# A hybrid attention trunk in fp32 on one core: block products chained in PSUM in the channel mixers, modulation sums in rows of 512 and moved to the first mixer

## The chip, the core and the metric

One core of a Trainium2 chip runs the whole kernel. The metric is device time in microseconds (us), the median of several executions; smaller is better. The engines are called here as in the profile: PE (TensorE, matrix products), DVE (VectorE), ACT (ScalarE), POOL (GpSimd) and SP (SyncE, which in this kernel issues all transfers).

## The reference, cut to what matters

The input x is 1 x 1024 x 1024 in float32. Two layers each run a token mixer (layer 0: softmax attention with forgetting; layer 1: gated linear attention) and a channel mixer. A conditioning vector c modulates every sub-layer with six vectors of 1024 per layer: shift, scale and gate of the token mixer (j = 0, 1, 2) and of the channel mixer (j = 3, 4, 5).

```python
c_act = jax.nn.silu(c)
for i in range(2):
    mod = c_act @ ada_w[i] + ada_b[i]              # 1024 -> 6 * 1024
    sh1, sc1, g1, sh2, sc2, g2 = jnp.split(mod, 6, axis=-1)
    h = modulate(rms_norm(x, norm1_g[i]), sh1, sc1)
    y = forgetting_attention(h, ...) if i == 0 else gated_linear_attention(h, ...)
    x = x + g1[:, None, :] * y
    h = modulate(rms_norm(x, norm2_g[i]), sh2, sc2)
    gate, up = jnp.split(h @ ffn_w_in[i], 2, axis=-1)
    x = x + g2[:, None, :] * ((jax.nn.silu(gate) * up) @ ffn_w_out[i])
return rms_norm(x, final_g)
```

The hidden width of the channel mixer is 2816.

## The kernel before, in words

**Products.** Everything is float32. An operand is split into a high part (a copy rounded to PE's fp32r format, made by ACT, line 174) and a low part (the difference, made by DVE, line 175); a product is three matmuls, high by high, high by low and low by high, added in one PSUM bank (`mm3`, lines 285 to 288).

**Order.** The program is written in one order, and a scheduler with a model of time then places each engine's instructions; each engine runs its own in the order so found. Some edges are fixed by hand with `issue_after`.

**Channel mixer.** `ffn` (from line 1380) works in blocks of 2 x 2: the activations are cut into B11, B12, B21, B22 (4 x 128 rows by 512 tokens), the weights likewise, and seven block products replace eight, with sums of blocks as operands: T1 to T4 on the side of the activations, made once, and sums of weight blocks, made by POOL for each group (lines 876, 877, 878, 888, 894). A *group* is one pair of 128-column weight strips: kind 0 for the gate, kind 1 for up; eleven of each, alternating. The first group of each kind is computed plainly (`plain_tile`), the other twenty with seven products (the loop from line 1678). A product (`prod`, line 1548) is 12 matmuls of 128 x 512 into a bank taken from a ring of five. Before the change each product leaves its bank at once: ACT copies the first to C11 (line 1684), DVE adds each of the others to one or two of the four results C11, C12, C21, C22 in SBUF (`add`, line 1557, L1559). Seven adds and one copy make a group. `fin` (line 1540) then applies silu on ACT (kind 0, L1543) or multiplies gate by up on POOL (kind 1, L1545), and `hid_done` sends the hidden block to memory some products later (split again at L1419 and L1420). The weight operands (`feed`) sit in a ring of six tiles and are loaded and split up to five ahead.

**Modulation.** The sum c_act @ ada_w is not done on PE, but on DVE: rows of ada_w are loaded to partitions, and each instruction multiplies a tile by a column of c_act (one value per partition) and adds it to an accumulator (`ada_steps`, lines 447 to 481; L475 the first, L477 the rest). Before the change a tile holds 32 rows of ada_w, each cut in four strips of 256 columns that lie on four groups of 32 partitions, so 32 instructions of 256 columns make one (layer, j), with four transfers per step (`ada_load`, L414). `ada_end` (L420) then sums over the partitions with two small matmuls against a constant of four columns, and DVE adds ada_b (L423).

When each (layer, j) is computed: (0, 0) and (0, 1) at the start by code that does not change; (0, 2), (0, 3), (0, 4) on DVE during attention, in steps of four rows per partition, paced by `ada0(2.4)` in `qk_proj`; (0, 5) on POOL during attention (`ada_pool`, L438 and L440), paced by `ada0p`; (1, 0) and (1, 1) in the first channel mixer, where each product gives a share of time to `ada1`; (1, 2), (1, 3), (1, 4) in the gated linear attention by `ada1(5.1)` after each projection; (1, 5) in the second channel mixer. `Pace` (line 483) counts the time given and lets the generators run as far as it reaches; `ADA_A` and `ADA_B` are the costs charged for one step.

**Attention** (L1165 to L1226): scores on PE, minimum and sum on DVE (L1171), exponential on ACT (L1175), reciprocal on DVE (L1176), scaling on POOL (L1177), transposes on PE (L1197), products with v (L1209, L1211). The projections of the next pair of heads are woven in between. **Gated linear attention**: per head, gates on ACT and DVE (L1891 to L1914), projections of k, q, v and r, and a chain of chunk states (from line 1948).

Of the kernel before, what the change touches and what calls it, by code (L numbers as in the profile page):

```python
# [53 lines left out]
def trunk(ctx, tc, x, c, ada_w, ada_b, norm1_g, norm2_g, ffn_w_in, ffn_w_out,  # L54
# [111 lines left out]
    four = cst.tile([P, 4], F32, name="four")  # L166
    nc.vector.memset(four, 0.0)
    for q in range(4):
        nc.vector.memset(four[32 * q:32 * q + 32, q:q + 1], 1.0)
# [115 lines left out]
    def mm3(ps, ah, al, bh, bl, start, stop):  # L285
        nc.tensor.matmul(ps, ah, bh, start=start, stop=False)  # L286
        nc.tensor.matmul(ps, ah, bl, start=False, stop=False)  # L287
        nc.tensor.matmul(ps, al, bh, start=False, stop=stop)  # L288
# [84 lines left out]
    crep = [crt[0:8, psl(t)] for t in range(4)] + [mrows[4][0:16, :], mrows[5][0:16, :]]  # L373
    for t in range(6):
        nt, src = (4, rows2[0:8, :]) if t < 4 else (2, crow)
        nc.vector.tensor_copy(crep[t].rearrange("n (q r) -> n q r", q=4),
                              src.rearrange("n (r t) -> n t r", t=nt)[:, t % 4].unsqueeze(1)
                              .to_broadcast([src.shape[0], 4, 32]))
    vps = mp0([P, 224], F32, "vps")
    vec = cst.tile([P, 160], F32, name="vec")  # L380
    cact = cst.tile([P, 8], F32, name="cact")
    c42 = cst.tile([P, 64], F32, name="c42")

    def vec_rows():
        nc.tensor.transpose(vps[:, 0:P], rows, ident)
        for t in range(6):
            n, o = (8, 160 + 8 * t) if t < 4 else (16, 128 + 16 * t)
            nc.tensor.transpose(vps[:, o:o + n], crep[t], ident[0:n, 0:n])
# [22 lines left out]
    def ada_load(raw, l, j, n, nt):  # L411
        src = ada_w[l, 32 * nt * n:32 * nt * (n + 1), j * D:(j + 1) * D]
        for q in range(4):
            nc.sync.dma_start(raw[32 * q:32 * q + 32],  # L414
                              src[:, 256 * q:256 * q + 256].rearrange("(r t) c -> r t c", t=nt))

    def ada_end(l, j, acc):
        mp = pj([P, 2, 4], F32, f"mp{l}{j}")
        for b in range(2):
            nc.tensor.matmul(mp[:, b], acc[:, psl(b)], four, start=True, stop=True)  # L420
        o = l * 48 + j * 8
        qb = lambda t: t.rearrange("p (q b) -> p b q", b=2)
# [5 lines left out]
    def ada_pool(l, j, acc, raw):  # L428

        raw = raw.rearrange("p (t c) -> p t c", t=2)  # L430
        ada_load(raw, l, j, 0, 2)
        yield 1.0
        for n in range(16):
            for t in range(2):
                o = 32 + t * 16 + n
                y = raw[:, t] if n or t else acc
                with tc.issue_after(last_of("G")):
                    nc.gpsimd.tensor_scalar(y, raw[:, t], c42[:, o:o + 1], 1.0, op0=ALU.mult, op1=ALU.mult)  # L438
                    if n or t:
                        nc.gpsimd.tensor_add(acc, acc, y)  # L440
                if t and n < 15:
                    ada_load(raw, l, j, n + 1, 2)
                yield 1.0
        ada_end(l, j, acc)
        yield 1.0

    def ada_steps(l, j, acc, raw_of, nt, ahead):


        steps, got = deque(range(32 // nt)), deque()  # L450

        def load():
            if not steps:
                return
            n = steps.popleft()
            raw = raw_of([P, nt * 256], F32, f"ada{l}{j}{n}").rearrange("p (t c) -> p t c", t=nt)
# [5 lines left out]
        for n in range(32 // nt):  # L462
            load()
            if ahead:
                yield ADA_A
            raw = got.popleft()
            with ExitStack() as es:
                if ahead:
                    es.enter_context(tc.issue_after(last_of("D")))
                elif n == 0:  # L470
                    es.enter_context(tc.issue_after(split_after["D"]))
                for t in range(nt):
                    o = (0 if nt == 4 else 32) + t * (32 // nt) + n
                    if n == t == 0:
                        nc.vector.tensor_scalar(acc, raw[:, t], c42[:, o:o + 1], None, op0=ALU.mult)  # L475
                    else:
                        nc.vector.scalar_tensor_tensor(acc, raw[:, t], c42[:, o:o + 1], acc,  # L477
                                                       op0=ALU.mult, op1=ALU.add)
            yield ADA_B if ahead else 1.0
        ada_end(l, j, acc)  # L480
        yield 1.0

# [22 lines left out]
    ada0, ada0p, ada1 = Pace(), Pace(), Pace()  # L505

    def ada1_queue(js, acc, raws_):
        r = Cycle(raws_)
        for j in js:
            ada1.q.append(ada_steps(1, j, acc, r, 2, len(raws_) - 1))  # L510
# [497 lines left out]
    nc.scalar.activation(c42, vps[:, 160:224], AF.Silu)  # L1008
# [121 lines left out]
    def qk_proj(p, i):  # L1130
# [9 lines left out]
        if p > 1:  # L1140
            ada0(2.4)
# [98 lines left out]
    def attention(p):  # L1240
        for a in range(2):
            for g in ORDER:
                u = (p, a, g)
                lps = yield from scores(u)
                if p:
                    ada0p(0.8)
# [29 lines left out]
    ada0p.flush()  # L1276
# [103 lines left out]
    def ffn(l, oh, xs, slots, nm, mid, norm_end, each=None):  # L1380
# [153 lines left out]
        TMP = {(0, 0): 0, (0, 1): 1, (1, 1): 2, (1, 0): 0}  # L1534
# [5 lines left out]
        def fin(G, key):  # L1540
            d = gate_view(G.i, key)
            if G.kind == 0:
                nc.scalar.activation(d, d, AF.Silu)  # L1543
                return
            nc.gpsimd.tensor_mul(d, d, dest(G, key))  # L1545
            hid_done(G.i, key)

        def prod(w, t):
            ps = pin([P, HALF], F32, f"p{l}")
            n = len(t)  # L1550
            for k in range(n):
                mm3(ps, w.hi[:, k, :], w.lo[:, k, :], hi(t[k]), lo(t[k]), k == 0, k == n - 1)
# [4 lines left out]
        def add(G, key, ps, src=None):  # L1557
            d = dest(G, key)
            nc.vector.tensor_add(d, d if src is None else dest(G, src), ps)  # L1559
# [118 lines left out]
        for X in gs[2:]:  # L1678
# [5 lines left out]
            nc.scalar.copy(dest(X, C11), prod(feed.next(), B11))  # L1684
            p5 = prod(feed.next(), T1)
            up(8)
            add(X, C12, prod(feed.next(), T2), C11)
# [114 lines left out]
    def mid(*js):  # L1802
        v = Views(slots["hid"], 2, [HALF], f"ad{js[0]}").v
        ada1_queue(js, v[0][:, 0:256], v[1:4])

    ADA_A, ADA_B = 6.0, 3.0
    ffn(0, oh, xs, slots, "fo", lambda: mid(0, 1), norm_mixer)
# [11 lines left out]
    vr = Ring(big, take(5))  # L1819
# [10 lines left out]
    ada_v = Views(take(2), 2, [HALF], "ad").v  # L1830
    ada1_queue((2, 3, 4), ada_v[0][:, 0:256], ada_v[1:3])
    ADA_A, ADA_B = 2.6, 1.0
    rm = ada_v[3]
# [33 lines left out]
    def gv_body(h, wv, tp, behind=None):  # L1867
# [5 lines left out]
        if h:  # L1873
            ada1(5.1)
# [43 lines left out]
    def head_front(h, b16, t2, ei, nmid):  # L1918
# [4 lines left out]
        for hf in range(2):  # L1923
# [3 lines left out]
            ada1(5.1)  # L1927
# [9 lines left out]
        for hf in range(2):  # L1937
# [3 lines left out]
            ada1(5.1)  # L1941
# [92 lines left out]
    def r_proj(h, gs, done):  # L2034
        wr_ = [None, None]
        for hf, dv in ((0, 0), (0, 1), (1, 0), (1, 1)) if h else ((0, 0), (1, 0), (0, 1), (1, 1)):
# [4 lines left out]
            ada1(5.1)  # L2041
# [58 lines left out]
    ada1.flush()  # L2100
# [50 lines left out]
    ffn(1, oh, xs, slots, "go", lambda: mid(5), final_norm, final_scale)  # L2151
# [30 lines left out]
```

## Time and profile before

| | us |
|---|---|
| median of 3 runs | 2394.64 |
| lowest and highest | 2393.22, 2395.78 |
| span of the profiled execution, first to last instruction | 2392.7 |

Only the span of the profiled execution is given, not its device time; the median of the runs is 1.9 us above it.

The stages by the profile's clock: loads, norm and first projections 0 to 95; attention 95 to 610; its output and the norm 610 to 686; first channel mixer, the seven-product groups with modulation 686 to 1040, the rest to 1310; gated linear attention 1310 to 1712; output and norm to 1768; second channel mixer 1768 to 2345; last norm and stores to 2393. A view by stages gives, for each stretch, its length, the busy time of each engine with its number of instructions, the granted TensorE clock (1.00 is full speed), the busy share of the DMA engines and the rate. A group's row has line, engine, operation, the tiles (out<-in), the shape, the count, then busy us and mean ns of one, then idle time before them and what ended it. In a chain or a timeline a row has start, length, and what ran.

### The profile page before, as it was taken

What the parts mean: (1) busy time and instruction counts of PE and PEld (TensorE: products, weight loads), DVE (VectorE), ACT (ScalarE), POOL (GpSimd) and SP (SyncE); (2) the same over time, 40 slices, a digit from 0 to 9 for tenths busy, and PEclk for the clock granted to TensorE, in tenths of its full rate; (3) what the DMA queues carried; (4) which work ended last, traced back from release to release, by engine and by line L of the source; (5) the groups of instructions that cost most, each with busy time, mean ns of one, the idle gap of its engine ahead of it and who ended that gap; (6) DMA issues with size and microseconds to landing.
All of it is one profiled execution on the core that took longest, in us unless ns stands there. A gap on an engine that the chain in (4) does not pass through costs nothing.

```text
span 2392.7 us, 35859 instructions
## 1 busy us (share of the span) xinstructions
PE 2367.3 (99%) x12344; PEld 2017.8 (84%) x12344; DVE 1770.0 (74%) x2984; ACT 1127.9 (47%) x2164; POOL 1046.2 (44%) x974
## 2 busy tenths in 40 slices
PE   8999999999999999999999999999999999999998
PEld 7888888888888888888888888898888888888888
DVE  6577787876698788876798565655687878775787
ACT  6656565664443333345325545453343334345326
POOL 1334444533446666643264221222345666643262
PEclk9999999999999999999999999999999999999999
DMA  7423333342435545457655242334424544457664
GB/s 254 151 79 112 102 119 93 121 142 78 150 113 178 176 162 168 168 203 266 223 183 161 68 119 87 100 113 132 143 99 154 183 150 154 154 186 258 227 199 147
DMA packets 336286, 363.43 MB, mean 152 GB/s; under 512 B 24860, under 2 KB 277944, under 8 KB 336104
## 3 DMA queue, kind: packets, MB, share of 16 engines
q1 hardware_dynamic: 336104, 361.15, 46.2%
q8 instruction: 97, 1.59, 0.3%
q14 instruction: 85, 0.70, 0.1%
HBM read 268.19 MB, written 92.86 MB: 151 GB/s over the span
## 4 chain that ended last, share of the span: by engine, by line
PE 89%; DVE 3%; DMA 3%; ACT 2%; issue 1%; SPq 1%; POOL 0%; DVEq 0%; POOLq 0%; ACTq 0%
PE p_b L288 16%; PE p_b L286 16%; PE p_b L287 16%; PE o_b L1211 2%; PE t_b L1197 2%; PE qk_b L286 2%; PE qk_b L287 2%; PE qk_b L288 2%; PE vps_b L288 1%; PE vps_b L286 1%; PE vps_b L287 1%; PE gr_b L286 1%; PE gr_b L287 1%; PE gr_b L288 1%; PE s_b L1165 1%; PE s_b L1166 1%
## 5 line engine op out<-in xcount | busy, mean ns | idle before, releaser
L175 DVE TENSOR_TENSOR o_s<-xv_s,o_s 128x512 fp32r<-128x512 f32 (+1 forms) x376 | 324.4, 868 | 62.8 <-ACT o_s L174 62.4
L174 ACT CAST o_s<-xv_s 128x512 fp32r<-128x512 f32 (+1 forms) x376 | 216.1, 587 | 293.9 <-PE p_b L288 242.3
L287 PE MATMUL p_b<-B,o_s 128*128 128x512 f32 x608 | 237.5, 391 | 0.0
L288 PE MATMUL p_b<-B,o_s 128*128 128x512 f32 x608 | 236.9, 390 | 0.0
L286 PE MATMUL p_b<-B,o_s 128*128 128x512 f32 x608 | 235.6, 391 | 0.0
L876 POOL TENSOR_TENSOR ex_s<-xv_s,xv_s 128x512 f32<-128x512 f32 (+1 forms) x64 | 86.8, 1357 | 288.0 <-DMA xv_s<-in_ffn_w_in_dram 118.2
L1177 POOL TENSOR_SCALAR lp_s<-lp_s,st 128x128 f32<-128x128 f32 (+7 forms) x128 | 97.5, 765 | 248.9 <-DVE st L1176 227.2
L286 PE MATMUL p_b<-T,o_s 128*128 128x512 f32 x480 | 186.7, 389 | 0.0
L287 PE MATMUL p_b<-T,o_s 128*128 128x512 f32 x480 | 186.7, 389 | 0.0
L288 PE MATMUL p_b<-T,o_s 128*128 128x512 f32 x480 | 181.2, 389 | 0.0
L288 PEld LDWEIGHTS p_b<-B,o_s 128*128 128x128 f32 x608 | 114.5, 188 | 23.8
L286 PEld LDWEIGHTS p_b<-B,o_s 128*128 128x128 f32 x608 | 114.6, 188 | 23.8
L287 PEld LDWEIGHTS p_b<-B,o_s 128*128 128x128 f32 x608 | 114.5, 188 | 23.8
L1175 ACT ACTIVATE lp_s<-lp_s,st 128x128 f32<-128x128 f32 (+7 forms) x128 | 99.3, 777 | 61.9 <-DVE st L1171 60.0
L878 POOL TENSOR_TENSOR xv_s<-ex_s,xv_s 128x512 f32<-128x512 f32 (+1 forms) x64 | 87.6, 1368 | 60.8 <-DVE o_s L175 58.2
L174 ACT CAST pt_s<-t_b 128x512 fp32r<-128x512 f32 (+1 forms) x160 | 79.8, 547 | 72.0 <-PE t_b L1197 71.4
L1559 DVE TENSOR_TENSOR ex_s<-ex_s,p_b 128x512 f32<-128x512 f32 x140 | 93.6, 680 | 25.1 <-PE p_b L288 24.9
L227 POOL TENSOR_TENSOR w_l_s<-w__s,w_h_s 128x256 fp32r<-128x256 f32 x90 | 69.3, 798 | 91.1 <-ACT w_h_s L223 51.9
L175 DVE TENSOR_TENSOR pt_s<-t_b,pt_s 128x512 fp32r<-128x512 f32 (+1 forms) x160 | 96.3, 630 | 15.7 <-ACT pt_s L174 15.2
L287 PEld LDWEIGHTS p_b<-T,o_s 128*128 128x128 f32 x480 | 90.1, 188 | 18.7
L286 PEld LDWEIGHTS p_b<-T,o_s 128*128 128x128 f32 x480 | 90.1, 188 | 18.7
L288 PEld LDWEIGHTS p_b<-T,o_s 128*128 128x128 f32 x480 | 90.1, 188 | 18.6
(1956 smaller groups left out, 7427.6 us busy)
## 6 DMA issues: line engine op xcount, KB each, us to landing
xv_s<-in_ffn_w_in_dram SPq DMA_DIRECT2D x176, 256.0 KB, 3.4
hid_B<-x SPq DMA_DIRECT2D x70, 512.0 KB, 2.9
ad_s<-in_ada_w_dram SPq DMA_DIRECT2D x384, 64.0 KB, 2.4
hid_T<-x SPq DMA_DIRECT2D x36, 512.0 KB, 2.9
xv_s<-in_ffn_w_out_dram SPq DMA_DIRECT2D x96, 192.0 KB, 5.0
ada_s<-in_ada_w_dram SPq DMA_DIRECT2D x96, 128.0 KB, 2.9
xv_s<-in_ffn_w_out_dram SPq DMA_DIRECT2D x40, 256.0 KB, 2.9
T2o<-hid_T SPq DMA_DIRECT2D x18, 512.0 KB, 8.8
```

What stands on the lines that cost most here:

```text
L174: nc.scalar.copy(hi, src)
L175: nc.vector.tensor_sub(lo, src, hi.bitcast(F32))
L227: (nc.gpsimd if i < 3 else nc.vector).tensor_sub(lo[:, cs], rw[:, cs], hi[:, cs].bitcast(F32))
L286: nc.tensor.matmul(ps, ah, bh, start=start, stop=False)
L287: nc.tensor.matmul(ps, ah, bl, start=False, stop=False)
L288: nc.tensor.matmul(ps, al, bh, start=False, stop=stop)
L876: nc.gpsimd.tensor_add(s1, a21, a22)
L878: nc.gpsimd.tensor_sub(a11, s1, a11)
L1175: nc.scalar.activation(lp, lp, AF.Exp, bias=mcur, scale=-1.0, accum_out=st[:, qi, 2:3])
L1177: nc.gpsimd.tensor_scalar(lp, lp, st[:, qi, 3:4], 1.0, op0=ALU.mult, op1=ALU.mult)
L1197: nc.tensor.transpose(tp[:, i, :], lps[qi][:, psl(2 * b + jj)], ident)
L1559: nc.vector.tensor_add(d, d if src is None else dest(G, src), ps)
```

## The change

In the channel mixers a product may go on in the bank of an earlier one. The bank `a` takes B11, T2, T3 and T4 in turn and is read after each; the bank `d` takes T1 and then B22. C11, C22 and C12 are first filled by ACT copies (three per group), three adds on DVE are left (C11, C22, C12), and C21 never lies in SBUF as a partial sum: kind 0 applies silu straight from the bank, kind 1 multiplies from the bank on DVE. A group takes three banks of the ring, not seven. The product with B22 is written ahead of that with T4, and two weight blocks change places in the order of loading.

Modulation tiles hold 64 rows by 512 columns on two groups of 64 partitions, so 16 instructions of 512 columns make one (layer, j), with two transfers per step; the constant has two columns, and the end takes four matmuls. POOL's sum is gone. (0, 5) and (1, 0) to (1, 4) are computed in the first channel mixer, with four buffers for raw rows in place of three; (0, 2) to (0, 4) stay in attention, in steps of two rows per partition; (1, 5) stays in the second channel mixer. In the gated linear attention the two slots that fall free give one more buffer for v.

```diff
     def ada_load(raw, l, j, n, nt):
-        src = ada_w[l, 32 * nt * n:32 * nt * (n + 1), j * D:(j + 1) * D]
-        for q in range(4):
-            nc.sync.dma_start(raw[32 * q:32 * q + 32],
-                              src[:, 256 * q:256 * q + 256].rearrange("(r t) c -> r t c", t=nt))
+        src = ada_w[l, 64 * nt * n:64 * nt * (n + 1), j * D:(j + 1) * D]
+        for q in range(2):
+            nc.sync.dma_start(raw[64 * q:64 * q + 64], src[:, hsl(q)].rearrange("(t r) c -> r t c", r=64))
 
     def ada_end(l, j, acc):
-        mp = pj([P, 2, 4], F32, f"mp{l}{j}")
-        for b in range(2):
-            nc.tensor.matmul(mp[:, b], acc[:, psl(b)], four, start=True, stop=True)
+        mp = pj([P, 4, 2], F32, f"mp{l}{j}")
+        for b in range(4):
+            nc.tensor.matmul(mp[:, b], acc[:, psl(b)], two, start=True, stop=True)
...
             yield ADA_B if ahead else 1.0
+        yield 5.0 if ahead else 1.0
         ada_end(l, j, acc)
...
-                r += [blk(a, A11), (op_a12, l, a), blk(a, A21, *then), blk(a, A22), blk(a, A12)]
+                r += [blk(a, A11), (op_a12, l, a), blk(a, A21, *then), blk(a, A12), blk(a, A22)]
...
-            ada0(2.4)
+            ada0(2.6)
...
-    acc0 = acc_r([P, 2, HALF], F32, "acc0")
-    ada0p.q.append(ada_pool(0, 5, acc0[:, 0, 256:512], acc0[:, 1]))
-    acc0 = acc0[:, 0, 0:256]
+    acc0 = acc_r([P, HALF], F32, "acc0")
     for j in (2, 3, 4):
-        ada0.q.append(ada_steps(0, j, acc0, wr, 4, 0))
+        ada0.q.append(ada_steps(0, j, acc0, wr, 2, 0))
...
-        def fin(G, key):
+        def fin(G, key, ps=None):
             d = gate_view(G.i, key)
             if G.kind == 0:
-                nc.scalar.activation(d, d, AF.Silu)
+                nc.scalar.activation(d, d if ps is None else ps, AF.Silu)
                 return
-            nc.gpsimd.tensor_mul(d, d, dest(G, key))
+            if ps is None:
+                nc.gpsimd.tensor_mul(d, d, dest(G, key))
+            else:
+                nc.vector.tensor_mul(d, d, ps)
             hid_done(G.i, key)
...
-            nc.scalar.copy(dest(X, C11), prod(feed.next(), B11))
-            p5 = prod(feed.next(), T1)
+            a = prod(feed.next(), B11)
+            nc.scalar.copy(dest(X, C11), a)
+            d = prod(feed.next(), T1)
+            nc.scalar.copy(dest(X, C22), d)
             up(8)
-            add(X, C12, prod(feed.next(), T2), C11)
+            prod(feed.next(), T2, a)
+            nc.scalar.copy(dest(X, C12), a)
             up(11)
             add(X, C11, prod(feed.next(), B21))
             fin(X, C11)
-            add(X, C22, prod(feed.next(), T3), C12)
-            add(X, C12, p5)
+            prod(feed.next(), T3, a)
+            add(X, C22, a)
+            fin(X, C22)
             up(15)
-            add(X, C21, prod(feed.next(), T4), C22)
-            fin(X, C21)
-            add(X, C22, p5)
-            fin(X, C22)
+            prod(feed.next(), B22, d)
+            add(X, C12, d)
+            fin(X, C12)
+            prod(feed.next(), T4, a)
+            fin(X, C21, a)
             up(20)
-            add(X, C12, prod(feed.next(), B22))
-            fin(X, C12)
             up(21)
...
-    ADA_A, ADA_B = 6.0, 3.0
-    ffn(0, oh, xs, slots, "fo", lambda: mid(0, 1), norm_mixer)
+    ADA_A, ADA_B = 2.0, 1.0
+    ffn(0, oh, xs, slots, "fo", lambda: mid(0, (0, 5), *((1, j) for j in range(5))), norm_mixer)
...
-    vr = Ring(big, take(5))
+    vr = Ring(big, take(6))
```

The calls `ada1(5.1)` after the projections of the gated linear attention are taken out, `ada_pool` and `ada0p` with them. `prod` takes an optional bank and then starts no new sum in it. At the start, one transposed block with c on 16 rows replaces six.

More of the change, by code (lines that the diff above doesn't have):

```diff
@@ L165, in trunk @@
     nc.vector.memset(mhalf, -0.5)
-    four = cst.tile([P, 4], F32, name="four")
-    nc.vector.memset(four, 0.0)
-    for q in range(4):
-        nc.vector.memset(four[32 * q:32 * q + 32, q:q + 1], 1.0)
+    two = cst.tile([P, 2], F32, name="two")
+    nc.vector.memset(two, 0.0)
+    for q in range(2):
+        nc.vector.memset(two[64 * q:64 * q + 64, q:q + 1], 1.0)
     maskb = cst.tile([P, P], BF16, name="maskb")
@@ L283, in next, with mm3 @@
             return self.got.popleft()
[L285 to L288, printed above, removed]
+    def mm3(ps, ah, al, bh, bl, start, stop, more=False):
+        nc.tensor.matmul(ps, ah, bh, start=start, stop=False, skip_group_check=more)
+        nc.tensor.matmul(ps, ah, bl, start=False, stop=False, skip_group_check=more)
+        nc.tensor.matmul(ps, al, bh, start=False, stop=stop, skip_group_check=more)
     def proj(ps, w, hs, hf):
@@ L426, in ada_end @@
                 make_a(l, i)
[L428 to L445, printed above, removed]
     def ada_steps(l, j, acc, raw_of, nt, ahead):
-        steps, got = deque(range(32 // nt)), deque()
+        steps, got = deque(range(16 // nt)), deque()
         def load():
@@ L461, in ada_steps @@
             load()
-        for n in range(32 // nt):
+        for n in range(16 // nt):
             load()
@@ L1555, in prod, with add @@
             return ps
-        def add(G, key, ps, src=None):
+        def add(G, key, ps):
             d = dest(G, key)
-            nc.vector.tensor_add(d, d if src is None else dest(G, src), ps)
+            nc.vector.tensor_add(d, d, ps)
         C11, C12, C21, C22 = (0, 0), (0, 1), (1, 0), (1, 1)
@@ L1829, in trunk @@
     s_slot, on_slot = take(2)
[L1830 to L1833, printed above, removed]
+    rm = Views(take(1), 2, [HALF], "rm").v[0]
     nc.vector.memset(rm, 1.0)
```

67 lines of the change are left out of this document (27 added, 40 removed).

## The prediction

> **What bounds the kernel now.** I read the first part of the page, then the busy time by stage, then what TensorE waited for, then the chain of waits where TensorE stood still.
>
> ```profile
> span 2392.7 us, 35859 instructions
> ...
> PE 2367.3 (99%) x12344; PEld 2017.8 (84%) x12344; DVE 1770.0 (74%) x2984; ACT 1127.9 (47%) x2164; POOL 1046.2 (44%) x974
> ```
>
> TensorE (PE) is busy in all but 25.4 us of the span, so a change that leaves its products alone can win no more than the holes, and each instruction added to PE is paid in full. The stages (us, then busy time of each engine, then the granted clock):
>
> ```profile
> core 0: us, PE busy (x) PEld busy (x) DVE busy (x) ACT busy (x) POOL busy (x), PEclk, DMA share, GB/s
> 0.00:95.00 95.00, 87.27 (x500) 77.14 (x501) 59.23 (x110) 63.50 (x98) 16.25 (x27) 0.98 0.68 221
> 95.00:610.00 515.00, 508.86 (x3261) 446.67 (x3260) 382.44 (x968) 307.70 (x654) 225.88 (x321) 1.00 0.34 106
> ...
> 686.00:1040.00 354.00, 354.00 (x1567) 293.17 (x1566) 294.72 (x384) 134.37 (x236) 217.08 (x144) 1.00 0.52 169
> 1040.00:1310.00 270.00, 269.70 (x1248) 225.66 (x1247) 206.54 (x294) 110.53 (x206) 115.42 (x95) 0.99 0.64 218
> 1310.00:1712.00 402.00, 398.52 (x2299) 349.73 (x2298) 244.01 (x434) 190.37 (x402) 102.69 (x124) 1.00 0.34 102
> ...
> 1768.00:2090.00 322.00, 322.00 (x1424) 266.65 (x1423) 256.59 (x322) 126.02 (x215) 200.83 (x132) 1.00 0.48 161
> 2090.00:2345.00 255.00, 254.17 (x1119) 209.56 (x1118) 188.72 (x263) 95.97 (x180) 109.91 (x86) 1.00 0.61 212
> 2345.00:2393.00 48.00, 40.75 (x310) 38.48 (x308) 34.64 (x61) 32.41 (x68) 16.00 (x13) 0.97 0.44 149
> ```
>
> The chained products stand in 686 to 1040 (first channel mixer) and 1768 to 2090 (second). There PE has no hole at all: 354.00 of 354 and 322.00 of 322, and a matmul every 354.00 / 1567 = 0.226 us. VectorE (DVE) is busy 83% beside it and GpSimd (POOL) 61%: both are hidden. Taking adds off VectorE there is worth **nothing by itself**. The holes that a shorter modulation could close lie in attention (95 to 610: 515 - 508.86 = 6.1 us) and in the gated linear attention (1310 to 1712: 402 - 398.52 = 3.5 us).
>
> Attention's largest hole, with the half-speed clock behind it:
>
> ```profile
> 409.45 0.50 DVE acc_s L477
> ...
> 411.34 2.98 DMA ada_s<-in_ada_w_dram
> 414.40 0.48 DVE acc_s L477
> ...
> 416.12 0.96 POOL lp_s L1177
> ```
>
> ```profile
> 412.00:424.00 12.00, 9.93 (x57) 8.72 (x56) 8.36 (x26) 6.29 (x15) 3.56 (x7) 0.86 0.52 157
> ```
>
> A modulation sum (L477) sits in VectorE's queue and waits for its rows of ada_w; the reciprocal behind it is late, then POOL's scaling of the attention weights, then the transposes. PE loses 12 - 9.93 = 2.1 us there, and the clock of 0.86 over 12 us takes 12 x 0.14 = 1.7 us more: 3.8 us. In the gated linear attention the hole is 1390 to 1404 (14 - 11.38 = 2.6 us):
>
> ```profile
> 1381.82 0.59 SPq L414
> 1382.51 3.95 DMA w__s<-in_gla_w_in_dram
> ...
> 1389.53 1.28 ACT L1899
> ```
>
> ```profile
> 1390.00:1404.00 14.00, 11.38 (x89) 10.60 (x88) 11.58 (x25) 9.81 (x21) 0.69 (x1) 1.00 0.28 81
> ```
>
> Four issues of ada_w (L414) stand on SyncE's queue ahead of the next head's weights; these land late, and the gate behind them (L1899) starts late.
>
> **The change, part by part.**
>
> *1. Modulation in attention.* POOL's sum for (0, 5) goes with its 64 transfers. The three on VectorE become 48 instructions of 512 columns in place of 96 of 256, and each step has two transfers where it had four. So less stands in front of L1176 and L1177. The hole at 412 hangs on exactly this: I take its 3.8 us as gone, and a quarter of the other 6.1 - 2.1 = 4.0 us: **-4.8 us**. Bounds: 0 (a two-row step still waits for its rows on VectorE; the same queue holds it) to -7.8 (all 6.1 and the 1.7).
>
> *2. Modulation in the gated linear attention* goes altogether: (1, 2) to (1, 4) with 96 sums and 192 transfers, each moved past the weights of that stage on SyncE's queue. The hole at 1390 goes; the rest hangs on other things: **-2.6 us**, bounds 0 and -3.5. The sixth buffer for v can only loosen waits here.
>
> *3. The end of each sum on PE* takes four matmuls against the new two-column constant, where it took two. One end before (four records, as each fp32 matmul makes two):
>
> ```profile
> 855.17 0.39 PE L287 MATMUL p_b<-T,o_s 128*128 128x512 f32 x1
> 855.40 0.50 PE L420 MATMUL mp_b<-four,ad_s 128*128 128x4 f32 x4
> 855.76 0.49 PE L288 MATMUL p_b<-T,o_s 128*128 128x512 f32 x1
> ```
>
> Four records hold PE from 855.40 to 855.76: 0.36 us. Four more per end cost as much to 0.45 us (the first of a run starts sooner than the rest); I take 0.4. Ten ends: **+4.0 us**, of it 6 x 0.76 - 2 x 0.36 = 3.8 in the first channel mixer, where nothing hides it, and -1.1 in the gated linear attention. The five small transposes that fall away at the start stand beside loads (a PE hole of 7.7 us in 0 to 95): 0.
>
> *4. Six sums in the first channel mixer.* VectorE in 686 to 1040, by form:
>
> ```profile
> L175 DVE TENSOR_TENSOR o_s<-xv_s,o_s 128x512 fp32r<-128x512 f32 x112 | 104.1, 931 | 7.5 <-ACT o_s L174 7.4
> L1559 DVE TENSOR_TENSOR ex_s<-ex_s,p_b 128x512 f32<-128x512 f32 x62 | 41.4, 679 | 4.3 <-PE p_b L288 4.2
> ...
> L1420 DVE TENSOR_TENSOR x<-x,x 128x512 fp32r<-128x512 f32 x22 | 25.6, 1163 | 21.2 <-ACT x L1419 20.9
> L477 DVE SCALAR_TENSOR_TENSOR ad_s<-ad_s,c,ad_s 128x256 f32<-128x256 f32 x41 | 24.7, 602 | 0.4
> L1559 DVE TENSOR_TENSOR x<-x,p_b 128x512 f32<-128x512 f32 x35 | 23.4, 677 | 3.8 <-PE p_b L288 3.8
> L1559 DVE TENSOR_TENSOR sg_s<-sg_s,p_b 128x512 f32<-128x512 f32 x28 | 18.6, 677 | 5.4 <-PE p_b L288 5.3
> L477 DVE SCALAR_TENSOR_TENSOR ad_s<-ad_s,c 128x256 f32<-128x256 f32 x21 | 13.0, 620 | 0.2
> ...
> L175 DVE TENSOR_TENSOR o009s_s<-ex_s,o009s_s 128x512 fp32r<-128x512 f32 x1 | 1.8, 1778 | 0.0
> ```
>
> The adds (L1559) take 41.4 + 23.4 + 18.6 = 83.4 us and fall by half: 14 in a pair of groups become 6 and one multiplication (-41.7). The sums of before (24.7 + 13.0 = 37.7, and 1.7 for two first ones) give way to 96 of 512 columns: 294.7 - 41.7 - 39.4 = 213.6 us, plus 96 times an unknown price. Bounds: 0.68 us (the 512-column adds above) and 1.778 us (the slowest 512-column instruction above). I take 0.93, L175's mean, which also reads two SBUF tensors: 303 us, 86% of 354, against 83%. VectorE stays hidden: 0, until the price passes (354 - 213.6) / 96 = 1.46 us. ScalarE gains two copies and POOL loses one of four multiplications per pair; both are below 62%.
>
> The L1559 rows read PSUM and hold 677 to 679 ns in every group, while L175 ranges up to 1778. The Trainium skill, GPSIMD Engine Reference, section 1 Specifications, says that GpSimd shares SBUF interfaces with VectorE and contends with VectorE instructions that read two SBUF tensors. The trace agrees, and the rule speaks against this part: it trades instructions that do not suffer for ones that do. By it the sums would stand nearer to L1420's 1163 ns: 213.6 + 112 = 325 us, 92%, still hidden.
>
> *5. The chain.* A bank that takes the next product must first be read. In the instruction order that the changed kernel is built to, products of neighbouring groups are interleaved, and between the end of a product and the next one on its bank stand 24 matmuls for the copy of C11 and of C22 (24 x 0.226 = 5.4 us), 22 for the copy of C12 (5.0), 23 for the add of C22 (5.2). The tightest is the last reader of a bank, before the ring gives it to the next group but one: 15 matmuls, 3.4 us. How late do readers come today?
>
> ```profile
> 866.79 0.39 PE L288 MATMUL p_b<-B,o_s 128*128 128x512 f32 x1
> ```
>
> ```profile
> 869.14 0.63 ACT L1543 ACTIVATE x<-x 128x512 f32<-128x512 f32 x1 [3.56 <-DVE x L1559]
> 870.34 0.63 ACT L1543 ACTIVATE x<-x 128x512 f32<-128x512 f32 x1 [0.57 <-DVE x L1559]
> 870.87 0.57 ACT L1684 COPY ex_s<-p_b 128x512 f32<-128x512 f32 x1
> ```
>
> The copy of C11 has its product at 867.18 and starts at 870.87, for ScalarE runs in order and waits with two activations for VectorE's adds. Late by 3.7 us and done 4.3 us after the product, it would fit under 5.4 us and miss 3.4. Behind the reader that PE waits for stand casts of later weights (L174) on ScalarE and their low parts (L175) on VectorE; before, banks had a ring of five to absorb that. I take **+1.5 us** in both mixers together; bounds 0 and +12 (0.3 us in each of 40 groups).
>
> **Sum**: -4.8 - 2.6 + 4.0 + 1.5 = -1.9 us on the span of 2392.7. The median of the runs stands 1.9 us above that span (2394.64), so I forecast **2392.7 us**.
>
> **The rivals.**
>
> *All holes close* (faster). Parts 1 and 2 at their far bounds, no wait in the chain: -7.8 - 3.5 + 4.0 = -7.3 us, 2387.3. For it: the two largest holes outside the start and the end have modulation in their chains. Against: other waits stand close behind (attention's DVE is 74% busy).
>
> *Late readers stop PE* (slower). In the mixers PE waits at the chained bank whenever its reader starts more than 3.4 - 0.7 = 2.7 us after the product. The 3.7 us above speaks for it; that most links have 5 us, against. At 12 us: -4.8 - 2.6 + 4.0 + 12 = +8.6, 2403. The Trainium skill, TensorE: Matmul & The Clock Gate, section "A second HAM failure mode: psum-queue depth-cycling", says that frequent small gaps between groups of matmuls make the clock gate fall back to half speed. The row at 412 agrees (0.86 behind a gap), the one at 1390 does not (2.6 us idle, clock 1.00). Each fall would cost about the 1.7 us of the row at 412.
>
> *VectorE becomes the bound in the first mixer* (slower): above 1.46 us a sum; at 1.778 us, 213.6 + 171 - 354 = 30 us over the stretch; -4.8 - 2.6 + 4.0 + 30 = +27, 2421.
>
> *The holes stay* (slower): attention and gated linear attention wait for something else at once, and only PE's extra work is left: +5.5, 2400.
>
> **How the numbers follow.** The forecast has 0.45, all holes closing 0.27, late readers 0.17, VectorE 0.05, holes that stay 0.06. A measurement of this kernel can tell about 0.2% (4.8 us) from no change. So faster 0.27, same 0.45, slower 0.28. The range reaches from just below the rival that closes all holes to past the one with late readers, 2386 to 2408; within 2390 to 2399 lies the forecast's own.
>
> **What would show it.** PE's hole at 412 and its 0.86 gone, and attention's idle time near 2 us (part 1). No L414 in 1310 to 1712 and idle time there below 1 us (part 2). Runs of eight records at the ends of sums, 0.7 to 0.8 us each (part 3). VectorE near 86% between 686 and 1040, and a 512-column sum near 0.93 us (part 4). PE's waits for ACT and DVE at p_b adding up to some 1.5 us (part 5). The forecast is wrong if PE waits at p_b in most groups, if the sums pass 1.46 us, or if attention keeps its 6 us.

## The result, and the profile after

The changed kernel takes 2415.19 us (median of four runs, 2412.82 to 2420.85) against 2395.21 us, a ratio of 1.0086 (95% interval 1.0071 to 1.0102): slower by some 20 us, outside the forecast's range. The profiled execution has a span of 2413.0 us, 20.3 us more than before.

The stages of before, read in the changed kernel (the first mixer is already late by 1040, and what follows it starts some 23 us later here, so the last two rows do not compare directly):

```profile
95.00:610.00 515.00, 510.30 (x3269) 445.77 (x3268) 368.69 (x918) 307.94 (x654) 189.95 (x258) 1.00 0.33 98
...
686.00:1040.00 354.00, 341.39 (x1508) 280.59 (x1507) 311.68 (x333) 144.87 (x257) 207.64 (x129) 0.99 0.64 200
1040.00:1310.00 270.00, 269.83 (x1201) 223.26 (x1200) 202.02 (x286) 107.50 (x202) 108.76 (x86) 1.00 0.66 223
1310.00:1712.00 402.00, 400.50 (x2361) 354.08 (x2360) 205.33 (x346) 197.34 (x414) 108.50 (x128) 1.00 0.24 75
```

In 686 to 1040 PE had no hole before; now it is idle for 354 - 341.39 = 12.6 us, at a mean clock of 0.99. To get rid of the shift I measured each stage in both traces from its own first matmul to its own last (p_b for a mixer):

| us | before | after | difference |
|---|---|---|---|
| start, to the first attention matmul | 76.4 | 76.6 | +0.2 |
| attention and its norm | 570.6 | 571.0 | +0.4 |
| first mixer | 601.3 | 624.5 | +23.2 |
| gated linear attention, from its first v product to the second mixer | 433.0 | 427.5 | -5.5 |
| second mixer | 603.2 | 605.3 | +2.1 |
| what follows the first mixer's p_b, and the end | 108.2 | 108.1 | -0.1 |

All of the loss is in the first mixer. Where PE waits there, by the view of waits (us in total, times, longest):

```profile
PE p_b L286 <- DVE x L1518: 7.7, 3, 5.2
PE p_b L286 <- DVE sg_s L1518: 2.7, 3, 1.1
PE mp_b L413 <- DVE ad_s L451: 2.2, 2, 1.5
```

L1518 is the new multiplication that reads C21 from its bank, the last reader of that bank: the rival with late readers, where it said. From the spacing of the matmuls (0.227 us where nothing waits) I add up the loss of the mixer: six gaps ahead of a product that waits for L1518, 11.4 us, and 0.6 us to get going again; 2.5 us where the end of a sum stands in PE's queue and waits for the sum; 2.2 us of half clock; the ends themselves 6 x 0.95 - 2 x 0.51 = 4.7 us (the time by which an end sets back the matmuls behind it, the restart of the stream included). One more fall of the clock to half, at 658 us behind 24 tiny matmuls of the norm, costs 1.6 us; those matmuls stood there before too, without a fall. That is 23.0 of 23.2.

The longest gap, from VectorE's side (timeline: start, length, line):

```profile
737.81 0.67 DVE L1534 TENSOR_TENSOR ex_s<-ex_s,p_b 128x512 f32<-128x512 f32 x1
738.41 1.45 DVE L1390 TENSOR_TENSOR x<-x,x 128x512 fp32r<-128x512 f32 x1
739.78 1.77 DVE L451 SCALAR_TENSOR_TENSOR ad_s<-ad_s,c,ad_s 128x512 f32<-128x512 f32 x1
741.47 3.46 DVE L175 TENSOR_TENSOR o_s<-xv_s,o_s 128x512 fp32r<-128x512 f32 x2
744.85 1.75 DVE L451 SCALAR_TENSOR_TENSOR ad_s<-ad_s,c,ad_s 128x512 f32<-128x512 f32 x1
746.52 1.75 DVE L1390 TENSOR_TENSOR x<-x,x 128x512 fp32r<-128x512 f32 x1
748.19 0.67 DVE L1518 TENSOR_TENSOR x<-x,p_b 128x512 f32<-128x512 f32 x1
```

VectorE has no idle moment, and what stands ahead of L1518 takes 1.45 to 1.77 us apiece where the same lines take 0.68 to 0.75 elsewhere. Those that read PSUM (L1534, L1518) keep 0.67. A second gap shows why; VectorE and, below it, GpSimd:

```profile
784.95 1.78 DVE L451 SCALAR_TENSOR_TENSOR ad_s<-ad_s,c 128x512 f32<-128x512 f32 x1
786.65 1.78 DVE L175 TENSOR_TENSOR o_s<-xv_s,o_s 128x512 fp32r<-128x512 f32 x1
788.35 1.78 DVE L451 SCALAR_TENSOR_TENSOR ad_s<-ad_s,c,ad_s 128x512 f32<-128x512 f32 x1
790.05 0.68 DVE L1390 TENSOR_TENSOR x<-sg_s,x 128x512 fp32r<-128x512 f32 x1
790.66 0.67 DVE L1518 TENSOR_TENSOR sg_s<-sg_s,p_b 128x512 f32<-128x512 f32 x1
```

```profile
784.45 1.73 POOL L1488 TENSOR_TENSOR sg_s<-sg_s 128x512 f32<-128x512 f32 x1
786.26 1.62 POOL L1489 TENSOR_TENSOR sg_s<-sg_s,sg_s 128x512 f32<-128x512 f32 x1
787.96 1.62 POOL L1494 TENSOR_TENSOR sg_s<-sg_s,sg_s 128x512 f32<-128x512 f32 x1
```

The two run in step, one VectorE instruction to each of GpSimd's; when GpSimd stops, VectorE is fast at once. By form, for the whole stretch:

```profile
L175 DVE TENSOR_TENSOR o_s<-xv_s,o_s 128x512 fp32r<-128x512 f32 x103 | 103.2, 1016 | 18.0 <-ACT o_s L174 17.8
L451 DVE SCALAR_TENSOR_TENSOR ad_s<-ad_s,c,ad_s 128x512 f32<-128x512 f32 x65 | 72.7, 1118 | 0.2
L1390 DVE TENSOR_TENSOR x<-sg_s,x 128x512 fp32r<-128x512 f32 x24 | 31.4, 1312 | 4.1 <-ACT x L1389 3.7
...
L451 DVE SCALAR_TENSOR_TENSOR ad_s<-ad_s,c 128x512 f32<-128x512 f32 x16 | 20.2, 1260 | 0.1
L1534 DVE TENSOR_TENSOR ex_s<-ex_s,p_b 128x512 f32<-128x512 f32 x24 | 15.7, 679 | 1.7 <-PE p_b L288 1.7
```

A sum costs (72.7 + 20.2) / 81 = 1.15 us. Sorted by whether a GpSimd operation ran beside it, some 40 sums with GpSimd idle take 736 to 752 ns, and 16 with GpSimd busy all along take 1670 to 1787.

The theories I set out with. **A**: the bank's last reader L1518 stands in VectorE's in-order queue behind moved sums that GpSimd slows; it alone is late. **B**: three chained banks per group in a ring of five are too tight whatever VectorE does. **C**: VectorE as a whole is behind, and any of its results will be late. **D**: the sums are slow for a reason of their own.

### The profile page after: what moved, and what is told of

Read it like the earlier page. It is cut to its first block, busy times and chain, and to the rows that moved or that the text cites. A ratio compares the mean times of both kernels' runs of the same rounds, so it can differ in the third digit from the quotient of the medians.

```text
span 2413.0 us, 35171 instructions
## 1 busy us (share of the span) xinstructions
PE 2374.7 (98%) x12379; PEld 2017.3 (84%) x12379; DVE 1736.1 (72%) x2709; ACT 1163.9 (48%) x2244; POOL 1007.7 (42%) x891
## 4 chain that ended last, share of the span: by engine, by line
PE 79%; DVE 8%; issue 4%; DMA 4%; ACT 2%; POOL 2%; SPq 1%; DVEq 0%; POOLq 0%; ACTq 0%
PE p_b L286 13%; PE p_b L287 13%; PE p_b L288 13%; PE o_b L1186 2%; PE t_b L1172 2%; DVE ad_s L451 2%; PE qk_b L286 2%; PE qk_b L287 1%; PE qk_b L288 1%; PE gr_b L286 1%; PE gr_b L287 1%; PE gr_b L288 1%; PE vps_b L288 1%; PE vps_b L286 1%; PE vps_b L287 1%
## 5 line engine op out<-in xcount | busy, mean ns | idle before, releaser
L175 DVE TENSOR_TENSOR o_s<-xv_s,o_s 128x512 fp32r<-128x512 f32 (+1 forms) x376 | 353.6, 955 | 108.3 <-ACT o_s L174 107.5
L286 PE MATMUL p_b<-T,o_s 128*128 128x512 f32 x480 | 187.2, 390 | 0.0
L287 PE MATMUL p_b<-T,o_s 128*128 128x512 f32 x480 | 186.8, 389 | 0.0
L288 PE MATMUL p_b<-T,o_s 128*128 128x512 f32 x480 | 186.7, 389 | 0.0
L1150 ACT ACTIVATE lp_s<-lp_s,st 128x128 f32<-128x128 f32 (+7 forms) x128 | 99.3, 776 | 73.6 <-DVE st L1146 72.7
L853 POOL TENSOR_TENSOR xv_s<-ex_s,xv_s 128x512 f32<-128x512 f32 (+1 forms) x64 | 93.3, 1458 | 45.4 <-DVE o_s L175 43.1
L863 POOL TENSOR_TENSOR xv_s<-xv_s,xv_s 128x512 f32<-128x512 f32 x40 | 68.4, 1711 | 103.7 <-issue 96.7
L175 DVE TENSOR_TENSOR pt_s<-t_b,pt_s 128x512 fp32r<-128x512 f32 (+1 forms) x160 | 95.8, 631 | 16.2 <-ACT pt_s L174 15.8
L288 PEld LDWEIGHTS p_b<-T,o_s 128*128 128x128 f32 x480 | 90.1, 188 | 18.8
```

The source lines that it names most:

```text
L175: nc.vector.tensor_sub(lo, src, hi.bitcast(F32))
L286: nc.tensor.matmul(ps, ah, bh, start=start, stop=False, skip_group_check=more)
L287: nc.tensor.matmul(ps, ah, bl, start=False, stop=False, skip_group_check=more)
L288: nc.tensor.matmul(ps, al, bh, start=False, stop=stop, skip_group_check=more)
L853: nc.gpsimd.tensor_sub(a11, s1, a11)
L863: nc.gpsimd.tensor_sub(r[A12], r[A12], r[A11])
```

## The experiments

Three groups, each timed beside the kernel before (2395.4, 2394.7 and 2394.6 us). "Mixer" below is first to last p_b matmul of the first mixer (601.3 us before, 624.5 after).

**The chain without the moved sums.**

```diff
-            add(X, C12, prod(feed.next(), T2), C11)
+            prod(feed.next(), T2, a)
+            nc.scalar.copy(dest(X, C12), a)
...
-    ffn(0, oh, xs, slots, "fo", lambda: mid(0, (0, 5), *((1, j) for j in range(5))), norm_mixer)
+    ffn(0, oh, xs, slots, "fo", lambda: mid(0, 1), norm_mixer)
```

(The first three lines stand for the whole chain, which is put in as in the change; the last two, read against the changed kernel, say that all modulation is that of before.)

> Only the chain of products is changed; all modulation stays as before the change (256-column sums, POOL's sum, two sums in the first mixer). Theory A (a bank's last reader, the multiplication of C21 on VectorE, is late because the moved sums stand ahead of it, each slowed by GpSimd): without the moved sums the first mixer's p_b part stays within 2 us of the 601.3 us of before, PE waits under 2 us for VectorE at p_b, and the whole is 2393 to 2398 us. Rival B (three chained banks a group in a ring of five are too tight whatever VectorE does): PE waits at p_b in most groups here too, the first mixer is 10 us or more longer, the whole 2404 us or more.

Measured: 2405.65 us, ratio 1.0038 (1.0024 to 1.0052); mixer 612.7, second mixer 603.3 (603.2 before). Theory A missed its number: with only two sums the chain still loses 11.4 us, most of it at L1548, which is what L1518 is in the changed kernel:

```profile
PE p_b L286 <- DVE x L1548: 5.6, 4, 3.7
```

But B doesn't hold either, since the same chain costs nothing in the second mixer. The tightest link leaves 3.24 us (worked out as the least time from the end of C21's product to the next product on its bank), so the reader must start within 2.6 us; its median start is 3.2 us after the product in the first mixer and 1.4 us in the second. Even the short sums were slow here, half of one form above 1.4 us (min/median/max):

```profile
L477 DVE SCALAR_TENSOR_TENSOR ad_s<-ad_s,c,ad_s x41: 470/485/1520, 712.4 to 1014.2; 128x256 f32<-128x256 f32 x41
L477 DVE SCALAR_TENSOR_TENSOR ad_s<-ad_s,c x21: 472/1402/1518, 701.5 to 1002.4; 128x256 f32<-128x256 f32 x21
```

**The moved sums without the chain.** The change's modulation, with the mixer's loop as before: seven adds and a copy per group.

```diff
-            prod(feed.next(), T2, a)
-            nc.scalar.copy(dest(X, C12), a)
+            add(X, C12, prod(feed.next(), T2), C11)
```

> Only the modulation is changed (rows of 512, six sums in the first mixer); every product leaves its bank at once as before the change. Theory A: VectorE, which keeps all its adds, gets 295 - 39 + 96 x 1.12 = 363 us of work in 354 us, so it falls behind in the first mixer: 2405 to 2425 us. Rival B (the chain does the harm, the sums none): only the six longer ends on PE cost, 4.7 us, against 5.4 us won in the gated linear attention: 2393 to 2398 us.

Measured: 2431.43 us, ratio 1.0149 (1.0135 to 1.0163); mixer 643.3. The sums do harm by themselves, more than theory A's 2425, and rival B falls. So the chain is not what makes the moved sums dear: it halves VectorE's adds and takes 18.8 us off their cost in the mixer (643.3 to 624.5). VectorE's busy time is no fuller than in the changed kernel, 311.4 of 354, and PE yet stands for 20 us:

```profile
686.00:1040.00 354.00, 334.12 (x1447) 271.19 (x1446) 311.38 (x375) 123.27 (x213) 198.03 (x127) 0.98 0.61 191
```

**A ring of seven banks.**

```diff
-        pin, pj = Ring(psp, bk[:5]), Ring(psp, bk[5:])
+        pin, pj = Ring(psp, bk[:7]), Ring(psp, bk[7:])
```

> The changed kernel with one number changed: the ring of banks for the products has seven banks, not five (two of the three that only the ends of the sums used). VectorE's work is the same. Theory A: a bank comes back about two thirds of a group later, PE's 11.3 us of gaps ahead of products that wait for the C21 multiplication go, and the 2.2 us of half clock with them; the waits at the ends of sums (2.5 us) and the ends (4.7 us) stay: 2400 to 2404 us. Rival C (VectorE is simply full in the first mixer, 312 of 354 us with waits between): a longer ring only delays the same stop, 2410 us or more.

Measured: 2424.65 us (2416.71 to 2427.38), ratio 1.0112 (1.0096 to 1.0127); mixer 624.0 in the profiled execution, the fastest of the five, as if nothing had been done. Theory A in its narrow form falls. PE no longer waits for the bank, it waits for other work of VectorE: the ends of sums, the low parts of weights.

```profile
PE mp_b L413 <- DVE ad_s L451: 9.0, 3, 4.0
PE p_b L288 <- DVE o_s L175: 1.5, 1, 1.5
PE p_b L286 <- DVE x L1534: 1.4, 2, 0.8
```

(The other banks that follow from this edit add 2 us ahead of the gated linear attention and 1.6 at the end; why its runs spread so far is open.)

**The sums in PSUM.** The accumulator of the mixers' sums is a PSUM bank, copied to SBUF once.

```diff
+                if n == 0:
+                    acc = pj([P, HALF], F32, f"pa{l}{j}")
...
+        if ahead:
+            nc.scalar.copy(sb, acc)
         yield 5.0 if ahead else 1.0
-        ada_end(l, j, acc)
+        ada_end(l, j, sb)
```

> The changed kernel, but the sums of the channel mixers are accumulated in a PSUM bank, so that each sum reads one SBUF tensor and one PSUM tensor where it read two SBUF tensors; ScalarE copies the result to SBUF at the end of each (six copies and one). The ring of five stays. Theory A: a sum falls from 1.12 us to about 0.7 us whatever GpSimd does (VectorE's work falls by 35 to 45 us), the queue ahead of the C21 multiplication is 1 us shorter for each sum in it, half or more of the 16.9 us of gaps go: 2398 to 2407 us. Rival D (the sums are slow for another reason, late rows or 512 columns as such): the sums stay at 1.1 us, and the time above 2411 us.

Measured: 2398.24 us, ratio 1.0014 (1.0005 to 1.0022); mixer 609.2; of the 7.9 us over before 4.7 are the ends and 3.2 are gaps. 17 of the 20 us are gone. The sum has one price now, whatever GpSimd does (min/median/max):

```profile
L454 DVE SCALAR_TENSOR_TENSOR pa_b<-ad_s,c,pa_b x90: 740/744/757, 713.3 to 1046.0; 128x512 f32<-128x512 f32 x90
```

In SBUF the same line ran from 736 to 1786. Rival D falls: neither the rows nor the 512 columns are at fault.

**The reader on ScalarE.**

```diff
-            if ps is None:
-                nc.gpsimd.tensor_mul(d, d, dest(G, key))
-            else:
-                nc.vector.tensor_mul(d, d, ps)
+            if ps is not None:
+                nc.scalar.copy(dest(G, key), ps)
+            nc.gpsimd.tensor_mul(d, d, dest(G, key))
```

> The changed kernel, but in the kind-1 groups ScalarE copies C21 out of its bank and GpSimd multiplies it with the gate; VectorE no longer reads that bank last. The sums and the ring of five stay. Theory A (the last reader of the bank stands in VectorE's queue behind instructions that GpSimd slows): PE's 11.3 us of gaps ahead of products that wait for the C21 multiplication and the 2.2 us of half clock go; the waits at the ends of sums (2.5 us) stay: 2400 to 2405 us. Rival C (VectorE is full and any of its results will be late): the gaps come back at another reader of VectorE, 2410 us or more.

Measured: 2415.05 us, ratio 1.0089 (1.0075 to 1.0103); mixer 626.2. As with seven banks the wait moves on, 5.0 us to the ends of sums, 2.7 us to low parts of weights. This edit gives GpSimd ten more multiplications (busy 215.5 us in 686 to 1040 in place of 207.6), so it would not settle the matter alone; but with seven banks that is two edits that free the bank and win nothing: the narrow A is dead. What is late is VectorE's queue, and the question is whether for the number of its instructions (C) or, call it **A2**, because those with two SBUF operands wait for GpSimd's.

**The chain alone, its sums in PSUM.** The first experiment, with PSUM accumulators as in the fourth.

```diff
-        ada1_queue(js, v[0][:, 0:256], v[1:4])
+        ada1_queue(js, v[0][:, 0:256], v[1:4], True)
...
+            if psum and n == 0:
+                acc = pj([P, 256], F32, f"pa{l}{j}")
```

> Only the chain is changed, all modulation as before the change, but the sums that lie in the channel mixers (two in the first, one in the second, 256 columns) are accumulated in a PSUM bank and copied to SBUF by ScalarE at the end. The chain alone took 2405.7 us. Theory A: the multiplication of C21 starts earlier, near the 1.4 us after its product that the second mixer shows, the first mixer loses its gaps but for 2 us: 2394 to 2399 us. Rival B (the chain is too tight in the first mixer also without slow sums): 2403 us or more.

Measured: 2393.49 us, ratio 0.9996 (0.9987 to 1.0005); mixer 601.3, exactly that of before, and no wait of PE at p_b is left. So the chain in a ring of five is not too tight; B falls for good. VectorE's mean load does not tell the two runs apart: with the chain alone it is busy 276.07 us of these 354 and PE stops, here 274.72 and PE does not, and before the change it was 294.72.

```profile
686.00:1040.00 354.00, 354.00 (x1567) 293.02 (x1566) 274.72 (x320) 155.12 (x275) 211.39 (x136) 1.00 0.52 168
```

**GpSimd idle.** The changed kernel with GpSimd's sums of weight and hidden blocks left out in the mixers (`op_sums`, `make_s4`, `op_s2`, `hid_done`); all else is there.

```diff
-        r["s"] = s1
-        nc.gpsimd.tensor_add(s1, a21, a22)
-        nc.gpsimd.tensor_sub(a21, a11, a21)
-        nc.gpsimd.tensor_sub(a11, s1, a11)
+        r["s"] = s1 = a21
...
```

> The changed kernel with GpSimd's sums of weight blocks and of hidden blocks left out in both channel mixers (the plain blocks stand in their place); GpSimd keeps only the multiplications of gate and up. VectorE's, ScalarE's and PE's instructions are all the same, the modulation sums lie in SBUF as before. Theory A2 (VectorE's instructions with two SBUF operands wait for GpSimd's, and that makes its queue late): a modulation sum falls from 1.15 us to below 0.85 us in the first mixer, PE's 16.9 us of gaps fall below 6 us: 2399 to 2406 us. Rival C (VectorE has simply too many instructions): the sums stay above 1.05 us and the time above 2411 us.

Measured: 2394.29 us, ratio 0.9999 (0.9990 to 1.0008), below the 2399 to 2406 us of theory A2; mixer 605.8, which is 4.4 us over before and about what the ends cost. In this stretch VectorE gets through more instructions than in the changed kernel (352 against 333, since nothing holds it up) and is busy 74 us less:

```profile
686.00:1040.00 354.00, 354.00 (x1583) 293.70 (x1582) 237.72 (x352) 150.73 (x269) 39.23 (x25) 1.00 0.67 212
```

```profile
L451 DVE SCALAR_TENSOR_TENSOR ad_s<-ad_s,c,ad_s x72: 737/746/1778, 702.1 to 1038.0; 128x512 f32<-128x512 f32 x72
L451 DVE SCALAR_TENSOR_TENSOR ad_s<-ad_s,c x18: 737/746/753, 708.3 to 1029.8; 128x512 f32<-128x512 f32 x18
```

All gaps are gone. By itself this run leaves a rival, for it also takes away the waits for GpSimd's results; but the sums in PSUM leave GpSimd all its work and win back 17 of the 20 us. The two together show the cause: not the number of VectorE's instructions, but GpSimd beside the sums that read two SBUF tensors.

**Looking for a better version.** The diffs of the sums in PSUM and of the reader on ScalarE at once:

> Both edits that bear on the late reader at once: the changed kernel with the 512-column sums of the mixers in PSUM (2398.2 us alone) and C21 of the kind-1 groups copied by ScalarE and multiplied by GpSimd (2415.1 us alone). Theory A2 (VectorE's queue is the cause, the reader only where it shows): of the 3.1 us of gaps that were left 1 to 2 us go, GpSimd's ten more multiplications cost nothing: 2395 to 2398 us. Rival (GpSimd's extra work slows VectorE's other instructions by as much): 2398 to 2403 us.

Measured: 2397.74 us, ratio 1.0012 (1.0003 to 1.0021); mixer 607.9. As expected, and not measurably better than PSUM alone. Then cheaper ends, from the chain alone with its sums in PSUM (256 columns, two matmuls an end): five sums in the first mixer, none in the gated linear attention (buffers, pace and the calls in that stage follow):

```diff
-    ffn(0, oh, xs, slots, "fo", lambda: mid(0, 1), norm_mixer)
+    ffn(0, oh, xs, slots, "fo", lambda: mid(0, 1, 2, 3, 4), norm_mixer)
```

> The chain; attention's modulation as before the change, with the sum on GpSimd; the five sums (1,0) to (1,4) in the first mixer, none in the gated linear attention; all sums of the mixers as 256 columns in a PSUM bank, ends with two small matmuls. Against the run with 512-column sums in PSUM (2398.2 us) PE has 5 x 0.46 us of ends in the first mixer in place of 6 x 0.94, and three cheaper ends in attention: theory A (PE's ends and late readers are all that is left to lose): 2391 to 2396 us, at or below the 2395.4 us of before. Rival (the 160 shorter sums with twice the transfers fill VectorE's queue again): 2400 us or more.

Measured: 2406.76 us, ratio 1.0052 (1.0039 to 1.0066); mixer 621.8. Missed: PE waits 9.9 us at the reader again, though a sum costs no more than 0.49 us. At its longest gap VectorE runs without a pause from 742.79 to 748.69 us, and there two L175 take 3.07 us and the low part of a hidden block 1.54 us: the PSUM accumulator spares the sums, not the other instructions with two SBUF operands. The same with the diff of the reader on ScalarE:

> The run with five 256-column sums in PSUM in the first mixer (2406.8 us), and C21 of the kind-1 groups copied by ScalarE. Its 13.4 us of gaps stood at the C21 multiplication on VectorE. If the reader alone was late there: 2392 to 2397 us, level with before. If VectorE's queue is late as a whole, as in the run with the reader on ScalarE and the sums in SBUF: 2403 us or more.

Measured: 2417.45 us, ratio 1.0090 (1.0076 to 1.0103); mixer 628.3: worse, with waits spread over VectorE and ScalarE. Why 160 sums of 256 columns fare so much worse than 96 of 512, with VectorE busy 291 us of 354 against 297, is open. No version here beats the kernel before by what can be measured.

**Attention without its sums.** The changed kernel; (0, 2) to (0, 4) are not computed, a constant stands for them.

```diff
-        ada0.q.append(ada_steps(0, j, acc0, wr, 2, 0))
+        nc.vector.memset(modc[:, 0, j], 0.5)
+    make_a(0, 1)
```

> The changed kernel with (0,2), (0,3) and (0,4) left out in attention: no loads, no sums, no ends; a constant stands in their place. My step on attention (its holes come from the modulation): the part from 95 to 610 us gains 3.6 us or more beside the 2.8 us of the three ends, the whole is 2408.5 us or less. Rival (attention waits for its own chain of softmax at once, and the sums' holes lie beside it): only the ends' 2.8 us or less go, 2412 us or more.

Measured: 2405.68 us, ratio 1.0051 (1.0037 to 1.0065). In the profiled execution attention and its norm take 564.7 us against 571.0: 2.9 us for the ends (3 x 0.95), 3.4 us for the sums. That is just short of the 3.6 us that my step asked for, and against the rival: the sums do cost attention something, and still do so in rows of 512. (The medians differ by 9.5 us, more than the 5.6 us of the two profiled spans; the profiled execution here is the slowest of its four.)

## Why the prediction was wrong, point by point

| term, us | forecast | measured |
|---|---|---|
| attention, without ends | -4.8 | -0.4 |
| gated linear attention, without ends | -2.6 | -4.0 |
| ends of the sums on PE | +4.0 | +4.5 |
| PE's waits in both mixers, with half clock | +1.5 | +20.1 |

(Ends at 0.95 and 0.51 us each, 0.45 apart; what the stage table leaves when they are taken off. Of the 20.1 us, 1.6 are the fall of the clock behind the norm, which no late reader causes.)

**1, attention: wrong.** The hole at 412 did close, as said:

```profile
412.00:424.00 12.00, 11.60 (x77) 9.61 (x75) 9.32 (x27) 6.60 (x16) 2.52 (x4) 1.00 0.48 134
```

PE has 11.60 of 12 us at full clock, where it had 9.93 at 0.86. But the time came back within the stage: the products that were 2.4 us behind before's pace ahead of that hole were level with it behind it, having lost those 2.4 us in small waits earlier, most of them between 270 and 310. So the hole was worth 2.4 us and not 3.8, and PE is still idle 515 - 510.30 = 4.7 us of the stage. I priced one hole and took it for the stage.

**2, gated linear attention: right**, and then some luck: 4.0 us, past my far bound of 3.5. Followed matmul by matmul, the hole at 1390 gave back 3.0 us, near the 2.6 I took. Another 1.5 us came at the start of the stage, where the kernel before had a spell of half clock (0.72 over 1300 to 1306) that the changed kernel lacks; why it does is open.

**3, ends: right**, 0.45 us more for each, the upper end of my 0.36 to 0.45.

**4, VectorE "stays hidden: 0": the step that failed.** The price was mis-sized, 1.15 us for 0.93, yet it was inside my bounds and below the 1.46 at which I let VectorE become the bound. The threshold itself was wrong. It compared sums over 354 us, where the queue fills in bursts:

```profile
735.00:748.00 13.00, 13.00 (x59) 10.74 (x59) 10.60 (x11) 3.91 (x7) 11.41 (x8) 1.00 0.51 177
735.00:748.00 13.00, 8.74 (x39) 6.91 (x37) 13.00 (x10) 4.30 (x9) 11.58 (x8) 0.94 0.48 162
```

The first row is the kernel before, the second the changed one. In these 13 us VectorE is now busy for 13.00 with ten instructions, where it was busy for 10.60 with eleven and PE had no gap; GpSimd is as busy as before, 11.58 against 11.41. At 88% on average (311.68 of 354) VectorE stops PE. None of the signs of being wrong that I had named came up as written: PE waited for L1518 six times in the twenty groups of the first mixer, not in most, and a sum stayed below 1.46 us.

**5, the chain: the mechanism right, the choice of +1.5 wrong.** The limit for the reader's start, 2.7 us, was right (2.6 from the trace), and so was the tightest link. I saw the copy of C11 late by 3.7 us and still chose a price near the low bound; the measured 20 us is beyond the far one of 12, and so are the 14.2 us of gaps, restart and half clock at L1518 in the first mixer alone. Nor was the link alone to blame: with seven banks or another reader the loss stayed.

**The rule I weighed and let go.** I quoted the contention with GpSimd and priced it at 1.16 us a sum, which was right, then asked only whether the mean fits. The Trainium skill, SBUF — State Buffer, section "Who interferes with whom", says more: the pair of ports that the two engines share is an exclusive lock; a VectorE instruction with two SBUF inputs contends with a GpSimd instruction that reads SBUF, and one with at most one SBUF input, outside the 2-port perf modes, does not. The trace agrees: a sum takes 1670 to 1787 ns beside a busy GpSimd, 736 to 752 without, 740 to 757 with the accumulator in PSUM.

**The clock.** In the seven-product groups of the first mixer it fell to half behind the longest gap alone, 5.57 us from one matmul's start to the next's; seven gaps of 0.85 to 1.88 us cost no clock. The chain of waits behind it shows the spacing of 0.43 in place of 0.23 us:

```profile
748.92 0.79 PE p_b L286
749.71 0.43 PE p_b L287
750.14 0.43 PE p_b L288
```

The fall cost 2.2 us, against my 1.7. The Trainium skill, TensorE: Matmul & The Clock Gate, section "HAM oscillation — how this bites in real kernels", sets the limit at idle gaps of some 3.4 us. The gaps of the changed kernel agree. The run with the sums alone does not: it had falls behind gaps of 2.5, 3.1, 3.3 and 4.3 us, and none behind one of 3.4, so here 3.4 us is no sharp limit for a single gap.

## What to carry to other kernels

An engine that runs in order bounds a stage when its queue is full for the length of the slack in front of its reader, so look at slices as short as that slack, not at the mean. VectorE work with two SBUF operands is to be priced by what GpSimd does beside it; an accumulator moved to PSUM takes the instruction out of the contest for one copy at the end (here that brought back 17 of 20 us with 96 sums; the version with 160 shorter ones still lost 12 us). When an edit frees one waiting resource and the time stays, look where the wait went: seven banks and another reader showed here that the queue was late, not the bank.

## What the runs showed of the hardware that was not expected

VectorE's 512-column fp32 instruction on two SBUF tensors takes 0.68 to 0.75 us alone and up to 1.8 us beside GpSimd; the sums beside a GpSimd that is busy all along take 1.67 to 1.79 us, in step with GpSimd's own 1.6 to 1.7 us. One with an operand in PSUM holds 0.67 to 0.76 us throughout. With GpSimd nearly idle (39 us busy in place of 208) VectorE is busy 238 us in place of 312, with more instructions done. The small fp32 matmuls that sum over the partitions set PE back by 0.95 us for four blocks against two columns, and by 0.51 us for two blocks against four.
